# Up-projection in quads: the two B22 products of two pairs by seven sub-products of 256 columns

## The chip, the cores and the metric

The kernel runs on one core of a Trainium2 chip. Its engines are TensorE (PE in the profile; PEld are its weight loads), VectorE (DVE), ScalarE (ACT), GpSimd (Pool) and SyncE (SP), which issues most of the DMAs. Each engine works its own queue of instructions in order and waits on semaphores for the others. The metric is the device time of the core in microseconds: the median of the runs, lower is better.

## The reference

One layer of a hybrid encoder over 1024 tokens of 1024 channels. The change is in its last part, the gated feed-forward network:

```python
def conv_gated_ffn(x, w_up, conv_w, conv_b, w_down):
    hu = x @ w_up                                   # 1024x1024 @ 1024x5632
    hc = conv_b + conv_w[2] * hu                    # causal depthwise conv, width 3
    for i in range(2):
        hc = hc + conv_w[i] * shift(hu, 2 - i)
    val, gate = jnp.split(hc, 2, axis=-1)
    return (jax.nn.gelu(gate, approximate=True) * val) @ w_down
```

## The kernel before

All arithmetic is float32. A float32 product is made of three matmuls: each operand is split into a high part (an fp32r copy, made by ACT, `wh`) and the low remainder (a subtraction on VectorE, `wl`), both in `split` (L78), and `mm3` (L84) issues high x high, high x low and low x high for each tile of 128 channels (a "k tile"). The weights are the stationary operand, the tokens the moving one.

The up-projection is worked in 22 pairs. A pair g is 128 value columns and the 128 gate columns that belong to them. Its 1024 x 256 weights and the 1024 x 1024 activations are each taken as a 2 x 2 block matrix, and the product is made by seven products of blocks in place of eight (`Pair`, `p1` to `p7`, in Winograd's form). The blocks of activations are B11, B21 and B22, the sums of them are T1 to T4; the sums of weights are s1 to s4. Each product has four k tiles, so 12 matmuls of 128 x 128 weights over 512 tokens, into one PSUM bank. `p3` is the product of s4 with B22: it is added in bank Y, to what p5 left there, and evicted with u2.

The order of a pair is p1, p2, p6, p3, p7, then p5 of the next pair, then p4 (`run_pair`). The weights' sums are made by `first` (s1) and `sums` (s2, s4, s3), on VectorE for g below 7 and on GpSimd from there (`V if g < 7 else G`). The splits run on ACT and VectorE a product or more ahead. Evictions to `hu` (L1183) are additions on VectorE, u2 (L260) and the copies of p1 and p5 are ACT's. After a pair, `conv` takes `hu` through an ACT pass (L1234) and two conv steps on VectorE (L1239); `gate` takes the GELU on ACT (L1244) and the product on VectorE (L1245), and stores to `g_d` in DRAM (the last two by a GpSimd DMA, the others by SP).

The start is written out by hand: pairs 0 and 1, whose first products run ahead, and p1 and p2 of pairs 2, 3 and 4, made ahead with results parked in DRAM (`e_d`), while the normalised activations `q` are turned in place into T1 to T4. Then comes the sequence 5, 2, 6, 3, 7, 4, 8, ... 21. A scheduler of the framework decides, at build time, where each instruction stands in its engine's queue; `tc.high_priority` and `tc.issue_after` steer it.

The down-projection (`prod(X, a11, b11, "p1", ...)` and on) follows on the same banks of TensorE. Its first products, p1, begin while the last pair is still gated; its p2 needs the loads a12 and b21, which SP issues (L1155) behind the loads that wait for gate 21's store.

Of the kernel before, what the change touches and what calls it, by code (L numbers as in the profile page):

```python
# [45 lines left out]
def trunk(ctx, tc, xn, xt, w_first, w_in, cols, gain_pre, bias, w_ao, w_pg, w_po, w_o, gains, w_up, w_dn, out):  # L46
# [1116 lines left out]
    with ExitStack() as ph:  # L1163
# [78 lines left out]
        def gate(g):  # L1242
# [8 lines left out]
        for at, g in enumerate(seq):  # L1251
            for n in seq[at + 1:at + 3]:
                if n not in raws and at:
                    load_wup(n)
            if at == NG - 4:
                for c in range(3):
                    load_chunk("a11", c)
            elif at >= NG - 2:
                load_chunk("b11", at - NG + 2)
            if g == 0:  # L1260
                new_hu(0)
                new_hu(1)
# [297 lines left out]
```

## Time and profile before

| | before |
|---|---|
| median of 3 runs | 1236.88 us (1236.60 to 1236.89) |
| profiled execution, span from first to last instruction | 1234.9 us |
| runs above that span | 2.0 us by the median (1236.88 - 1234.9); no other time of that execution is recorded |
| TensorE clock granted, mean | 0.998 |
| TensorE matmuls | 5743 |
| up-projection on TensorE | about 595 to 1017 us of the span |
| down-projection | from 1017.41 us on |

How to read the rows that follow in the prediction: a page row of a group gives line, engine, operation, tiles out<-in (buffer numbers left out), shape and count, then the busy time in us, the mean of one in ns, and the idle time ahead of it with what ended it. A row of the timeline gives start and duration in us. A row of stretches gives from:to, length, and the busy time and count of PE, PEld, DVE, ACT and POOL, then the granted clock, the share of the DMA engines and GB/s. Matmuls are pipelined, so their pace is the distance of their starts, not their durations; the same holds for short operations on VectorE.

### The profile page before, as it was taken

The page shows a single profiled execution, that of the slowest core. Times are in us where ns is not written, and L with a number is a line of the kernel's source. Part 1 is how long each engine was busy: PE and PEld are TensorE (multiplying, and loading weights), DVE is VectorE, ACT ScalarE, POOL GpSimd, SP SyncE. Part 2 cuts the span into 40 slices and gives each one's busy share as a digit, 9 for nine tenths or more (in the row PEclk, how much of TensorE's full clock was granted, in tenths as well). Part 3 has the DMA queues.
Part 4 walks back from the last instruction along what each step waited for, and adds up shares of the span by engine and source line. Part 5 has one row for each costly group of instructions (what it writes and reads, how often), then busy time and mean ns, then how long its engine had stood idle before and what let it go on. Part 6 is the DMA issues. An engine that isn't in the chain of part 4 may idle for free.

```text
span 1234.9 us, 16242 instructions
## 1 busy us (share of the span) xinstructions
PE 1225.3 (99%) x5743; PEld 1020.9 (83%) x5743; DVE 949.6 (77%) x1551; ACT 667.2 (54%) x1171; POOL 211.0 (17%) x183
## 2 busy tenths in 40 slices
PE   9999999999999999999999999999999999999997
PEld 7888888888889987888888888888888888888886
DVE  5898677866788878756799887667666675999968
ACT  6764355555577773434546555554545455445553
POOL 0000000043254545000000112433333300000000
PEclk9999999999999999999999999999999999999999
DMA  9879245438886845322352232222132127902103
GB/s 329 333 256 350 85 147 207 154 124 264 291 276 214 264 178 207 137 86 76 113 196 111 111 145 103 71 84 102 52 102 85 61 68 255 350 18 103 34 1 137
DMA packets 63857, 193.84 MB, mean 157 GB/s; under 512 B 6048, under 2 KB 6688, under 8 KB 58656
## 3 DMA queue, kind: packets, MB, share of 16 engines
q1 hardware_dynamic: 55712, 176.55, 40.8%
q10 hardware_dynamic: 7056, 12.59, 2.7%
q0 software_dynamic: 1008, 3.67, 0.7%
q8 instruction: 45, 0.74, 0.2%
q14 instruction: 36, 0.29, 0.1%
HBM read 139.84 MB, written 52.95 MB: 156 GB/s over the span
## 4 chain that ended last, share of the span: by engine, by line
PE 92%; DVE 6%; issue 1%; DMA 0%; ACT 0%; POOL 0%; DVEq 0%; ACTq 0%
PE X_u L84 19%; PE X_i L84 12%; PE Y_u L84 10%; PE Y_i L84 9%; PE X L84 7%; PE wops L1115 7%; PE Z_u L84 4%; PE y L84 4%; PE ybp L84 4%; PE Y L84 4%; PE f L916 3%; PE tp L891 2%; PE Z_i L84 2%; PE first L466 2%; PE pst L848 1%; DVE a L1405 1%
## 5 line engine op out<-in xcount | busy, mean ns | idle before, releaser
L1239 DVE SCALAR_TENSOR_TENSOR hc<-hu,cv,hc 128x1022 f32<-128x1022 f32 (+1 forms) x88 | 115.6, 1315 | 27.7 <-ACT hc L1234 27.7
L78 ACT CAST wh_u<-s_u 128x512 fp32r<-128x512 f32 x88 | 54.4, 619 | 90.2 <-PE Y_u L84 47.7
L78 DVE TENSOR_TENSOR wl_u<-s_u,wh_u 128x512 fp32r<-128x512 f32 x88 | 62.4, 711 | 33.9 <-ACT wh_u L78 33.9
L78 ACT CAST wh_i<-s_i 128x512 fp32r<-128x512 f32 x64 | 39.8, 622 | 75.9 <-PE X_i L84 36.0
L78 ACT CAST wh_u<-wup 128x512 fp32r<-128x512 f32 x60 | 37.3, 621 | 52.0 <-PE X_u L84 27.5
L78 DVE TENSOR_TENSOR wl_i<-s_i,wh_i 128x512 fp32r<-128x512 f32 x64 | 46.2, 722 | 21.3 <-ACT wh_i L78 16.3
L1234 ACT ACTIVATE hc<-hu,cv 128x1024 f32<-128x1024 f32 x44 | 54.6, 1244 | 9.8 <-DVE hu L1183 8.9
L202 POOL TENSOR_TENSOR s_i<-win 128x512 f32<-128x512 f32 x4 | 5.9, 1481 | 257.0 <-DVE wl_i L78 246.6
L202 POOL TENSOR_TENSOR s_u<-wup 128x512 f32<-128x512 f32 x15 | 25.7, 1713 | 139.4 <-DVE wl_u L78 139.4
L78 DVE TENSOR_TENSOR ptl<-tp,pth 128x512 fp32r<-128x512 f32 (+3 forms) x80 | 42.8, 552 | 7.7 <-ACT pth L78 7.2
L866 ACT ACTIVATE pe<-sm,st 128x640 f32<-128x640 f32 (+2 forms) x64 | 44.3, 695 | 7.7 <-DVE st L864 7.5
L870 POOL TENSOR_SCALAR pe<-pe,st 128x640 f32<-128x640 f32 (+4 forms) x58 | 40.7, 705 | 44.2 <-DVE st L868 30.0
L78 ACT CAST pth<-tp 128x512 fp32r<-128x512 f32 (+3 forms) x80 | 36.3, 474 | 15.9 <-PE tp L891 11.0
L78 DVE TENSOR_TENSOR wl_u<-wup,wh_u 128x512 fp32r<-128x512 f32 x60 | 43.0, 719 | 1.2 <-ACT wh_u L78 0.5
L84 PE MATMUL ybp<-mx,wh_yb 128*128 128x512 f32 x128 | 43.3, 412 | 0.0
L1244 ACT ACTIVATE hc<-hc 128x1024 f32<-128x1024 f32 x22 | 23.4, 1062 | 36.9 <-DVE hc L1239 36.9
L864 DVE CUSTOM_DVE_ANT_0 sm<-pst,bt 128x640 f32<-128x640 f32 (+2 forms) x64 | 40.7, 651 | 3.0 <-issue 1.7
L206 POOL TENSOR_TENSOR s_u<-s_u,wup 128x512 f32<-128x512 f32 x15 | 19.4, 1291 | 102.3 <-DVE wl_u L78 99.6
L916 PE MATMUL f<-pth,vv 128*128 128x256 f32 x144 | 36.6, 286 | 0.0
L916 PE MATMUL f<-ptl,vv 128*128 128x256 f32 x144 | 36.5, 287 | 0.0
L208 POOL TENSOR_TENSOR s_u<-wup 128x512 f32<-128x512 f32 x15 | 32.2, 2144 | 23.5 <-DVE wl_u L78 23.5
L891 PE MATMUL tp<-ident,pe 128*128 128x128 f32 x240 | 35.3, 274 | 0.2
(523 smaller groups left out, 4135.7 us busy)
## 6 DMA issues: line engine op xcount, KB each, us to landing
wup<-in_w_up SPq DMA_DIRECT2D x22, 1024.0 KB, 5.0
win<-in_w_in SPq DMA_DIRECT2D x16, 1024.0 KB, 7.0
g_d<-hc SPq DMA_DIRECT2D x20, 512.0 KB, 2.6
sig_d<-d ACTq DMA_DIRECT2D x32, 256.0 KB, 2.0
a<-g_d SPq DMA_DIRECT2D x8, 1024.0 KB, 11.4
b<-in_w_dn SPq DMA_DIRECT2D x8, 1024.0 KB, 12.7
w<-in_w_in SPq DMA_DIRECT2D x12, 512.0 KB, 7.3
x<-in_xn SPq DMA_DIRECT2D x8, 512.0 KB, 8.5
```

What stands on the lines that cost most here:

```text
L78: return A.copy(hi, src), (eng or V).tensor_tensor(lo, src, hi.bitcast(F32), ALU.subtract)
L84: nc.tensor.matmul(ps, a[i], b[i], start=start and i == 0 and p == 0, stop=stop and i == n - 1 and p == 2, skip_group_check=True,)
L202: self.eng.tensor_tensor(self.s1, self.w21, self.w22, ALU.add)
L208: self.eng.tensor_tensor(self.s3, self.w11, self.w21, ALU.subtract)
L864: V.tensor_tensor_reduce(so, sv, bv, -1.0, 3e38, ALU.add, ALU.min, st[:, 0:1])
L866: A.activation(pe[:, :n], sm[:, :n], AF.Exp, scale=-1.0, bias=st[:, 0:1], accum_out=st[:, 1:2])
L870: (V if 4 * h + J in (0, 1, 31) else G).tensor_scalar(pe[:, :n], pe[:, :n], st[:, 2:3], 1.0, ALU.mult, ALU.mult)
L891: nc.tensor.transpose(tp[:, c * P:(c + 1) * P], pe[:, b * P:(b + 1) * P], ident)
L916: nc.tensor.matmul(fo, vv[:, kb, e].rearrange("p a d -> p (a d)"), t[:, s], start=s == slots[0] and x == 0, stop=s == slots[-1] and x == 1)
L1115: nc.tensor.matmul(ps[:, 512 * c:512 * c + 512], a[k // 4][:, k % 4, sl], wo[k][b][:, 512 * c:512 * c + 512], start=k == 0 and x == 0, sto ...
L1234: A.activation(c, hu, AF.Identity, scale=cv[:, C_CW + 88 + b:C_CW + 89 + b], bias=cv[:, C_CB + b:C_CB + b + 1])
L1239: V.scalar_tensor_tensor(c[:, n:], hu[:, :S - n], cv[:, w:w + 1], c[:, n:], ALU.mult, ALU.add)
```

## The change

Pairs are worked two at a time, in quads: (0,1), (5,2), (6,3), (7,4), (8,9) ... (20,21). The order in a quad of pairs a and b is p1 a, p2 a, p1 b, p2 b, p6 a, p6 b, then both p3, then p7 a, p7 b, p5 of the next quad's two pairs, p4 a, p4 b. Pairs 2, 3 and 4 have no p1 and p2 there.

The two products s4(a) B22 and s4(b) B22 together are a 2 x 2 block product of their own: two rows of weights (a, b), two halves of channels (two k tiles each), two halves of tokens (256 columns each). In quads 1 to 9 they are made by seven sub-products of two k tiles and 256 columns, six matmuls each (`third`), 42 matmuls where there were 24 of 512. The right operands are quarters of B22 and of a new operand E22, whose four quarters are differences of quarters of B22, made once on GpSimd (`quarters`) and split once on ACT and VectorE, in two `raw` buffers. The left operands are halves of s4 of a and b (splits q3a, and q3d for a half) and four sums of such halves (`third_weights`, `third_sums`, each of 256 columns on GpSimd), split again (q3e, q3b). Four sub-products go directly into the banks Y of a and b; three go into two further banks (r, q), are copied to `cc` by ACT, and added to both u2 by GpSimd (L1298, L1301) and VectorE (L1304, from the bank). The first and the last quad keep `p3`.

`sums` writes s3 over w21, and `fourth` s4 over w12, so a pair has tiles of its own for s1 and s2 only. `cc` shares the three buffers of `hc`. The weights of pairs 5 and 2 are loaded over q[0,0] and q[1,1] once these are free; afterwards both pairs of the next quad are loaded at the start of a quad. The conv and gate calls of both pairs of a quad stand in the next quad; those of pairs 20 and 21 stand at the end. The parked p1 of pairs 2, 3 and 4 is loaded one pair at a time.

```diff
+            def sums(self):
+                self.s2 = self.st("s2")
+                self.eng.tensor_tensor(self.s2, self.s1, self.w11, ALU.subtract)
+                self.s3 = self.w21
+                self.eng.tensor_tensor(self.s3, self.w11, self.w21, ALU.subtract)
+            def fourth(self):
+                self.s4 = self.w12
+                self.eng.tensor_tensor(self.s4, self.w12, self.s2, ALU.subtract)
...
+        def load_over(g, t):
+            raws[g] = t.rearrange("p k n -> p (k n)")
+            nc.sync.dma_start(raws[g], w_up[g])
...
+        def third_weights(a, b):
+            A4, B4 = a.s4, b.s4
+            wA = split_w(A4, f"q3a_{a.name}")
+            wt = [wsp.tile([P, 4, P], F32R, tag=x, name=f"{x}_q3d_{a.name}") for x in ("wh", "wl")]
+            w22 = [x[:, 0:2] for x in wt]
+            split(w22[0], w22[1], B4[:, 2:4])
+            G.tensor_tensor(B4[:, 2:4], B4[:, 0:2], B4[:, 2:4], ALU.add)
+            return wA, w22
+        def third_sums(a, b):
+            A4, B4 = a.s4, b.s4
+            G.tensor_tensor(B4[:, 0:2], A4[:, 0:2], B4[:, 0:2], ALU.subtract)
+            G.tensor_tensor(A4[:, 0:2], B4[:, 2:4], A4[:, 0:2], ALU.subtract)
+            G.tensor_tensor(A4[:, 2:4], A4[:, 2:4], A4[:, 0:2], ALU.subtract)
+        def third(a, b, wA, w22):
+            wA2 = split_w(a.s4, f"q3e_{a.name}")
+            wB2 = split_w(b.s4, f"q3b_{a.name}")
+            w11, w12 = [[x[:, i:i + 2] for x in wA] for i in (0, 2)]
+            s2, s4 = [[x[:, i:i + 2] for x in wA2] for i in (0, 2)]
+            s3, s1 = [[x[:, i:i + 2] for x in wB2] for i in (0, 2)]
+            B, E = Tu["B22"], Tu["E22"]
+            r, q7 = [psu.tile([P, 512], F32, tag="m", name=f"{n}_{a.name}")[:, :256] for n in ("r", "q")]
+            cc = tmp.tile([P, 4, 256], F32, tag="hc", name=f"cc_{a.name}", bufs=3)
+            u2 = a.quad["u2"]
+            two = u2.rearrange("p f (c n) -> p f c n", c=2)
+            lo, hi = slice(0, 256), slice(256, 512)
+            eighths(r, w11, quarter(B, "11"), True, True)
+            with tc.high_priority():
+                A.copy(cc[:, 0], r)
+            eighths(b.Y[:, lo], w22, quarter(E, "21"), False, True)
+            eighths(a.Y[:, lo], w12, quarter(B, "21"), False, True)
+            eighths(r, s2, quarter(E, "22"), False, True)
+            with tc.high_priority():
+                A.copy(cc[:, 1], r)
+            G.tensor_tensor(two[:, :, 0], two[:, :, 0], cc[:, 0:2], ALU.add)
+            eighths(q7, s3, quarter(E, "12"), True, True)
+            A.copy(cc[:, 2], q7)
+            G.tensor_tensor(two[:, 1], two[:, 1], cc[:, 2:3].to_broadcast([P, 2, 256]), ALU.add)
+            eighths(a.Y[:, hi], s4, quarter(B, "22"), False, True)
+            eighths(r, s1, quarter(E, "11"), False, True)
+            V.tensor_tensor(two[:, :, 1], two[:, :, 1], r.unsqueeze(1).to_broadcast([P, 2, 256]), ALU.add)
+            a.evict(0, 1, a.Y, a.u2)
+            b.evict(0, 1, b.Y, b.u2)
...
+        quarters = [q[1, 1][:, k:k + 2, c:c + 256] for k in (0, 2) for c in (0, 256)]
+        for o, x, y in ((0, 1, 0), (1, 3, 1), (3, 3, 0), (2, 2, 3)):
+            G.tensor_tensor(quarters[o], quarters[x], quarters[y], ALU.subtract)
...
+        e22 = [rawp.tile([P, 4, 512], F32R, tag="raw", name=f"E22{x}") for x in "hl"]
+        for c in range(4):
+            split(e22[0][:, c], e22[1][:, c], q[1, 1][:, c])
+        Tu["E22"] = e22
+        load_over(2, q[1, 1])
+        p0.p7(False)
+        pair = pair_up(5), es[2]
+        pair[0].first()
...
+            a.p1()
+            if n == 1:
+                with tc.issue_after(gate(0).ins):
+                    for g in nxt:
+                        load_wup(g)
+                conv(1, 0)
+            else:
+                conv(u, 1)
+            a.p2()
+            a.fourth()
+            if n == 1:
+                conv(1, 1)
+            else:
+                gate(u)
+                conv(v, 1)
+            if not begun:
+                b.p1()
+                b.p2()
+            if n == 1:
+                b.first()
+                b.sums()
+                b.p5()
+            b.fourth()
+            a.p6()
+            gate(v)
+            if not final:
+                wts = third_weights(a, b)
+                third_sums(a, b)
+            b.p6()
+            if final:
+                a.p3()
+                b.p3()
+            else:
+                third(a, b, *wts)
+                after = []
+                for g in nxt:
+                    if g in es:
+                        es[g].weights(raws[g])
+                    after.append(es[g] if g in es else pair_up(g))
+                after[0].first()
+            a.p7(False)
+            conv(gs[0], 0)
+            if not final:
+                after[0].sums()
+                after[1].first()
+            b.p7(False)
+            if not final:
+                after[0].p5()
+                after[1].sums()
+                conv(gs[1], 0)
+                after[1].p5()
+            else:
+                conv(gs[1], 0)
+            a.p4(False)
+            if final:
+                conv(gs[0], 1)
+                gate(gs[0])
+            b.p4(False)
```

The first place is VectorE at the entry of quad 1. The names: u5 and u2 are the pairs, `wup2` or `h2_11` hold pair 2's weights, `h2_00` pair 5's; a name ends in a buffer's number. Before, from the low half of s2 of pair 5 (wl_6_u5, for its p6) to that of s1 of pair 2 (wl_5_u2, for its p5):

```order
L78 TENSOR_TENSOR wl_6_u5_6620<-s2_u5_6495,wh_6_u5_6619 128x512
L78 TENSOR_TENSOR wl_3_u5_6640<-s4_u5_6496,wh_3_u5_6639 128x512
L1245 TENSOR_TENSOR hc0_0_6554<-hc0_0_6554,hc0_1_6558 128x1024
L78 TENSOR_TENSOR wl_7_u5_6657<-s3_u5_6497,wh_7_u5_6656 128x512
L1183 TENSOR_TENSOR hu5_0_6613<-Z_u5_6596,p1_u5_6567 128x512
L206 TENSOR_TENSOR s2_u2_6677<-s1_u2_6616,wup2_6562 128x512
L1239 SCALAR_TENSOR_TENSOR hc1_1_6592<-hu1_1_6129,cv_76,hc1_1_6592 128x1022
L207 TENSOR_TENSOR s4_u2_6678<-wup2_6562,s2_u2_6677 128x512
L1239 SCALAR_TENSOR_TENSOR hc1_1_6592<-hu1_1_6129,cv_76,hc1_1_6592 128x1023
L208 TENSOR_TENSOR s3_u2_6679<-wup2_6562 128x512
L78 TENSOR_TENSOR wl_5_u2_6686<-s1_u2_6616,wh_5_u2_6685 128x512
```

And now the rows from pair 5's s4 to gate 1's product:

```order
L1215 TENSOR_TENSOR h2_00_5305<-h2_00_5305,s2_u5_6502 128x512
L202 TENSOR_TENSOR s1_u2_6624<-h2_11_5308 128x512
L1364 TENSOR_TENSOR hc0_0_6558<-hc0_0_6558,hc0_1_6562 128x1024
L1209 TENSOR_TENSOR s2_u2_6626<-s1_u2_6624,h2_11_5308 128x512
L1183 TENSOR_TENSOR hu5_0_6617<-X_u5_6600,p1_u5_6571 128x512
L1211 TENSOR_TENSOR h2_11_5308<-h2_11_5308 128x512
L1358 SCALAR_TENSOR_TENSOR hc1_1_6620<-hu1_1_6129,cv_76,hc1_1_6620 128x1022
L78 TENSOR_TENSOR wl_5_u2_6632<-s1_u2_6624,wh_5_u2_6631 128x512
L1358 SCALAR_TENSOR_TENSOR hc1_1_6620<-hu1_1_6129,cv_76,hc1_1_6620 128x1023
L1215 TENSOR_TENSOR h2_11_5308<-h2_11_5308,s2_u2_6626 128x512
L78 TENSOR_TENSOR wl_6_u5_6651<-s2_u5_6502,wh_6_u5_6650 128x512
L1364 TENSOR_TENSOR hc1_0_6596<-hc1_0_6596,hc1_1_6620 128x1024
```

wl_5_u2 stood ten rows behind wl_6_u5 and stands three ahead of it; s1, s2 and s3 of pair 2 moved ahead of it with it.

The second place is GpSimd in the steady part, one quad. Before, the s1, s2, s4 and s3 of pair 9 (L202, L206, L207, L208), and on with pair 10 in the same pattern:

```order
L202 TENSOR_TENSOR s1_u9_7402<-wup9_7243 128x512
L206 TENSOR_TENSOR s2_u9_7463<-s1_u9_7402,wup9_7243 128x512
L207 TENSOR_TENSOR s4_u9_7464<-wup9_7243,s2_u9_7463 128x512
L208 TENSOR_TENSOR s3_u9_7465<-wup9_7243 128x512
L202 TENSOR_TENSOR s1_u10_7550<-wup10_7357 128x512
```

And now, in quad (10, 11), up to its last two operations (L1209 is s2, L1215 s4, L1211 s3, L1267 to L1275 the sums of the halves of s4; u12 and u13 are the next quad's pairs):

```order
L202 TENSOR_TENSOR s1_u12_8018<-wup12_7814 128x512
L1211 TENSOR_TENSOR wup12_7814<-wup12_7814 128x512
L1215 TENSOR_TENSOR wup11_7486<-wup11_7486,s2_u11_7754 128x512
L1209 TENSOR_TENSOR s2_u12_8042<-s1_u12_8018,wup12_7814 128x512
L1267 TENSOR_TENSOR wup11_7486<-wup11_7486 128x256
L1273 TENSOR_TENSOR wup11_7486<-wup10_7484,wup11_7486 128x256
L1274 TENSOR_TENSOR wup10_7484<-wup11_7486,wup10_7484 128x256
L1275 TENSOR_TENSOR wup10_7484<-wup10_7484 128x256
L202 TENSOR_TENSOR s1_u13_8045<-wup13_7816 128x512
L1211 TENSOR_TENSOR wup13_7816<-wup13_7816 128x512
L1298 TENSOR_TENSOR u2_u10_7907<-u2_u10_7907,cc_u10_7967 128x2x256
L1301 TENSOR_TENSOR u2_u10_7907<-u2_u10_7907,cc_u10_7967 128x512
```

The sums of halves and the two additions to u2 (L1298, L1301) came in between, the latter behind s1 and s3 of the next quad's second pair.

The third place is VectorE at the end of the up-projection, from the last conv step of the last gate's half to that gate's product; p1a and p1b are operands of the down-projection's p1. Before, of pair 21:

```order
L1239 SCALAR_TENSOR_TENSOR hc21_1_9427<-hu21_1_9330,cv_76,hc21_1_9427 128x1022
L1239 SCALAR_TENSOR_TENSOR hc21_1_9427<-hu21_1_9330,cv_76,hc21_1_9427 128x1023
L78 TENSOR_TENSOR wl_p1a2_9521<-a11_0_8839,wh_p1a2_9520 128x512
L78 TENSOR_TENSOR wl_p1a3_9541<-a11_0_8839,wh_p1a3_9540 128x512
L1245 TENSOR_TENSOR hc21_0_9389<-hc21_0_9389,hc21_1_9427 128x1024
```

And now, beginning with the last conv step and the product of gate 20:

```order
L1358 SCALAR_TENSOR_TENSOR hc20_1_9696<-hu20_1_9651,cv_76,hc20_1_9696 128x1023
L1364 TENSOR_TENSOR hc20_0_9653<-hc20_0_9653,hc20_1_9696 128x1024
L78 TENSOR_TENSOR wl_p1a2_9830<-a11_0_9138,wh_p1a2_9829 128x512
L78 TENSOR_TENSOR wl_p1a3_9850<-a11_0_9138,wh_p1a3_9849 128x512
L1358 SCALAR_TENSOR_TENSOR hc21_1_9736<-hu21_1_9673,cv_76,hc21_1_9736 128x1022
L78 TENSOR_TENSOR wl_p1a4_9870<-a11_1_9140,wh_p1a4_9869 128x512
L1358 SCALAR_TENSOR_TENSOR hc21_1_9736<-hu21_1_9673,cv_76,hc21_1_9736 128x1023
L78 TENSOR_TENSOR wl_p1a5_9890<-a11_1_9140,wh_p1a5_9889 128x512
L78 TENSOR_TENSOR wl_p1a6_9910<-a11_1_9140,wh_p1a6_9909 128x512
L78 TENSOR_TENSOR bl_p1b4_9874<-b11_1_9472,bh_p1b4_9873 128x512
L1364 TENSOR_TENSOR hc21_0_9675<-hc21_0_9675,hc21_1_9736 128x1024
```

Gate 20's product and five more splits of the down-projection stand ahead of gate 21's product now, one of them, bl_p1b4, for that p1's fifth k tile.

More of the change, by code (lines that the diff above doesn't have):

```diff
@@ L1231, in conv @@
             b = g + NG * f
-            hu = hus[g][f]
+            hu = hus[g, f]
             c = hcs[g, f] = tmp.tile([P, S], F32, tag="hc", name=f"hc{g}_{f}", bufs=3)
@@ L1367, in trunk @@
+            if not final:
+                pair = after
+        with tc.high_priority():
+            pre = [(split_a(blk["a11"][k], f"p1a{k}"), split_a(blk["b11"][k], f"p1b{k}")) for k in range(2)]
+        conv(gs[1], 1)
+        gate(gs[1])
     upp.close()
```

265 lines of the change are left out of this document (147 added, 118 removed).

## Prediction

> **What bounds the kernel now.** I read the page's busy times first, then the chain that ended last, then busy times by stretch.
>
> ```profile
> span 1234.9 us, 16242 instructions
> PE 1225.3 (99%) x5743; PEld 1020.9 (83%) x5743; DVE 949.6 (77%) x1551; ACT 667.2 (54%) x1171; POOL 211.0 (17%) x183
> ...
> PE 92%; DVE 6%; issue 1%; DMA 0%; ACT 0%; POOL 0%; DVEq 0%; ACTq 0%
> ...
> 595.00:1017.00 422.00, 421.97 (x1873) 348.93 (x1872) 323.40 (x391) 227.42 (x330) 98.99 (x62) 1.00 0.28 97
> 640.00:660.00 20.00, 20.00 (x90) 16.57 (x89) 19.73 (x27) 10.14 (x14) 0.00 (x0) 1.00 0.49 177
> 660.00:680.00 20.00, 20.00 (x90) 16.57 (x89) 19.89 (x27) 11.05 (x17) 0.00 (x0) 1.00 0.35 122
> 680.00:700.00 20.00, 20.00 (x90) 16.58 (x89) 17.73 (x22) 11.55 (x18) 1.28 (x1) 1.00 0.28 106
> 760.00:798.00 38.00, 38.00 (x169) 31.46 (x168) 25.55 (x30) 19.45 (x29) 13.29 (x9) 1.00 0.24 83
> ```
>
> The columns of a stretch are its length, then the busy time of PE, PEld, DVE, ACT and POOL. TensorE makes 99% of the span, and in the up-projection (595 to 1017 us) it idles 0.03 us in 422, at full clock (1.00). So a matmul that goes is time that goes, as long as nothing starts to be late. How much the others have left differs by stretch: from 760 on, two pairs take 38 us and VectorE has 12.5 us free; between 640 and 680, where pairs 0 and 1 run out and pair 5 begins, VectorE has 0.38 us free in 40. The two stretches are judged apart.
>
> **The matmuls: removed 24, added 42, per quad.** The start times of a 12-matmul product (its first matmul, and that of the next product), then two rows each of two runs of 256-column matmuls in the attention, which load new weights for each matmul as the new ones do (PEld has as many instructions as PE):
>
> ```profile
> 837.89 0.39 PE L84 MATMUL Y_u<-B22h,wh_u 128*128 128x512 f32 x1
> ...
> 840.61 0.39 PE L84 MATMUL X_u<-T3h,wh_u 128*128 128x512 f32 x1
> 439.64 0.28 PE L916 MATMUL f<-ptl,vv 128*128 128x256 f32 x1
> ...
> 440.78 0.28 PE L916 MATMUL f<-ptl,vv 128*128 128x256 f32 x1
> 376.19 0.28 PE L916 MATMUL f<-pth,vv 128*128 128x256 f32 x1
> ...
> 377.49 0.28 PE L916 MATMUL f<-ptl,vv 128*128 128x256 f32 x1
> ```
>
> A product takes 2.72 us, 0.227 a matmul. The first run has ten distances in 1.14 us (0.114), the second eleven in 1.30 (0.118); I take 0.116. Two products were 5.44 us; 42 matmuls are 42 x 0.116 = 4.87 us: 0.57 us less. Quads 1 to 9 are worked so (the first and the last keep p3): 9 x 0.57 = **5.2 us gained**; by 0.118 it is 4.4, by 0.114 5.9. From 0.130 on nothing is gained.
>
> **The start, quad 1 (pairs 5 and 2).** Pair 2's s1, s2, s3 and product p5 now stand ahead of pair 5's p6; before, p5 came three products (8 us) later, behind pair 5's p6, p3 and p7. Four splits of E22 (four 512-column subtractions on VectorE) come before them, and the load of pair 2's weights, on SP, waits for these. VectorE's durations:
>
> ```profile
> 640.20 0.68 DVE L258 TENSOR_TENSOR u_u<-X_u,hu 128x512 f32<-128x512 f32 x1
> 640.80 0.68 DVE L202 TENSOR_TENSOR s_u<-wup 128x512 f32<-128x512 f32 x1
> ...
> 652.58 3.67 DVE L1239 SCALAR_TENSOR_TENSOR hc<-hu,cv,hc 128x1022 f32<-128x1022 f32 x3
> 656.16 0.69 DVE L1183 TENSOR_TENSOR hu<-X_u,hu 128x512 f32<-128x512 f32 x1
> ...
> 659.16 1.22 DVE L1245 TENSOR_TENSOR hc<-hc,hc 128x1024 f32<-128x1024 f32 x1
> 660.29 0.68 DVE L78 TENSOR_TENSOR wl_u<-s_u,wh_u 128x512 fp32r<-128x512 f32 x1
> 661.05 0.69 DVE L1183 TENSOR_TENSOR hu<-Z_u,p_u 128x512 f32<-128x512 f32 x1
> ...
> 665.85 0.68 DVE L78 TENSOR_TENSOR wl_u<-s_u,wh_u 128x512 fp32r<-128x512 f32 x1
> ```
>
> From start to start a 512-column operation takes 0.60, a conv step 1.19 (3.58 / 3), a gate product 1.13. After the operation of 640.20 the new queue holds, up to and with wl_5 of pair 2, 23 operations of 512 (four of them E22), seven conv steps and one gate product: 23 x 0.60 + 7 x 1.19 + 1.13 = 23.3 us from 640.8, so wl_5 is there at 664.1 (before: 666.5, the row of 665.85). TensorE ends pair 5's p2 at about 660.9 (the eviction of 661.05 waited for it). Its new order fills in with two matmuls of each of four products whose high half is there (2 x 0.227 + 2 x 0.227 + 4 x 0.116 = 1.4), until 662.3, and then waits for wl_5: **1.8 us**. Next, ten matmuls later (666.4), it needs wl_6 of pair 5, which stands behind a conv step and two more operations: 664.1 + 1.19 + 3 x 0.60 = 667.1 at most; I take 0.2 for it, as each operation's result counts from its own end. Sum **2.0 us lost, once**. Nothing gives it back: TensorE has no later idle time. Ends: 0 (if VectorE runs these in another rhythm), 5.5 (the new Pool sums at their slowest, 4 x 0.98 us later than I count, below, which would make wl_q3e late). I stay at the queue's sum. The third's splits come in time by this count: wl_q3d ends at 668.8, Pool's four sums of 256 columns take half of L206's 1.29 each (671.4), ACT and VectorE some 0.6 each with a start between (672.8); wl_q3e is wanted at 673.2, after pair 2's p6 (671.6) and the sub-products ahead. The c1 halves are now loaded one by one (three of 256 KB); the DMA queues were busy 0.35 to 0.49 there, so I cost that at nothing.
>
> **The steady quads.** Per quad come 1.5 splits, three copies of 256 columns on ACT, one addition with PSUM on VectorE (L1304), and on Pool four operations of 256 and two of 512 columns (L1298, L1301). VectorE's 1.5 x 0.60 + 0.60 = 1.5 us go into 12.5 us of free time; ACT's into 18. Pool's are the question, since L1298 and L1301 stand in a chain: copy of r, L1298, L1301, L1304, and behind L1304 on VectorE everything that leads to wl_4.
>
> ```profile
> L206 POOL TENSOR_TENSOR s_u<-s_u,wup 128x512 f32<-128x512 f32 x15 | 19.4, 1291 | 102.3 <-DVE wl_u L78 99.6
> L202 POOL TENSOR_TENSOR s_u<-wup 128x512 f32<-128x512 f32 x15 | 25.7, 1713 | 139.4 <-DVE wl_u L78 139.4
> L208 POOL TENSOR_TENSOR s_u<-wup 128x512 f32<-128x512 f32 x15 | 32.2, 2144 | 23.5 <-DVE wl_u L78 23.5
> 664.07 0.58 ACT L260 COPY u_u<-X_u 128x512 f32<-128x512 f32 x1
> ```
>
> Count from a.p1 (T = 0), with products of 2.72: six products and the third's first four sub-products (24 x 0.116) end at 19.1, the copy of r at most 0.58 later, 19.7. L1298 and L1301 at 1.29 each: 22.3. L1304 22.9; wl_5 of the next pair, two evictions and that of a.p7, 4 x 0.60: 25.3; ACT's conv of a began after the first of these evictions (24.1) and takes 1.25 (the page's L1234 group has a mean of 1244 ns, quoted below), so conv step a 25.4 to 26.6; conv step b, an eviction, two conv steps and wl_4: 26.6 + 1.19 + 0.60 + 2.38 + 0.60 = 31.4; with hand-overs of some 0.05 us I take 31.7. TensorE wants wl_4 at 21.2 + 4 x 2.72 + 2 x 0.227 = 32.5. **Margin 0.8 us, cost 0.** Of the Pool rows I take L206's, since L1298 too waits for another engine and is then free to start; behind it in Pool's queue stand L1301 and the next pair's s2 and s4, wanted many us later. Ends: no loss, or both operations as long as L208's (2.14, at single rows 2.27): 2 x 0.98 - 0.8 = 1.2 us a quad, 10.4 in all. Why L208 is slow:
>
> ```profile
> L1234 ACT ACTIVATE hc<-hu,cv 128x1024 f32<-128x1024 f32 x44 | 54.6, 1244 | 9.8 <-DVE hu L1183 8.9
> 796.25 2.27 POOL L208 TENSOR_TENSOR s_u<-wup 128x512 f32<-128x512 f32 x1 [1.76 <-DVE wl_u L78]
> ...
> 796.09 1.27 DVE L1239 SCALAR_TENSOR_TENSOR hc<-hu,cv,hc 128x1023 f32<-128x1023 f32 x1
> ```
>
> It starts 0.16 us into a conv step on VectorE, which ends at 797.36, and takes 1.16 us from there: as if it had waited for that end. In the new order wl_7 and wl_5 splits stand on VectorE at T = 19 to 22, not conv steps, and they wait for TensorE; so a Pool operation can meet one of 0.6 us. [...]
>
> **The tail.** Gates 20 and 21 both come at the end, and SP's loads of the down-projection stand behind them.
>
> ```profile
> 1017.41 0.39 PE L84 MATMUL X<-wh_p1b,wh_p1a 128*128 128x512 f32 x1
> ...
> 1023.63 1.22 DVE L1245 TENSOR_TENSOR hc<-hc,hc 128x1024 f32<-128x1024 f32 x1
> ...
> 1032.32 0.92 SPq L1155 DMA_DIRECT2D a<-g_d  x2
> ...
> 1039.75 0.62 ACT L78 CAST wh_p2a<-a 128x512 fp32r<-128x512 f32 x1 [2.15 <-DMA a<-g_d]
> ...
> 1047.37 0.39 PE L84 MATMUL Y<-bh_p2b,wh_p2a 128*128 128x512 f32 x1
> ```
>
> Gate 21's product came 6.2 us after the down-projection's start; by the new queue (gate 20, two splits, a conv step, a split, a conv step, three splits ahead of it) it comes at about 11. The store and the loads behind it, b21 and a12, move 4.9 us with it: a12 is there at 1044.6, split by 1046.0, wanted at 1047.4. Cost **0**, margin 1.4; the other end is 2.
>
> **Sum**, against the profiled execution: span 1234.9 - 5.2 + 2.0 = 1231.7 us. The runs' median, 1236.88, lies 2.0 above that span; the same lies around the new one: **1233.7 us**.
>
> **Rivals.** *Pool in the chain (slower).* Decides from a loss of 3.2 / 9 = 0.36 us a quad, i.e. when L1298 and L1301 take over 1.29 + (0.8 + 0.36) / 2 = 1.87 us each. At L208's 2.27 the time is 1233.7 + 10.4 = 1244.1. For it: two of the three Pool rows are above 1.7. Against: what stands beside them on VectorE. *Half of it (no change).* At 1.8 us each: 2 x 0.51 - 0.8 = 0.2 a quad, 2 us; with a further 1 us at quad 1 or in the tail, 1236.7. For it: three places with margins of 0.4 to 1.4 us. *The narrow matmuls do not do what they say.* If 42 loads of weights, each before only 256 columns, do not hide, the distance is above 0.130 and nothing is gained: 1236.9 + 2.0 = 1238.9. At PEld's mean of 178 ns (1020.9 / 5743) it would be 42 x 0.178 - 5.44 = 2.0 us more a quad, 1257. Against: both quoted runs. [...]
>
> **Chances.** Forecast 0.5, Pool 0.18, half of it 0.22, narrow matmuls 0.1. What differs by under 0.2% (2.5 us) cannot be told from no change here. The forecast's gain is 3.2, so a fifth of its cases count as no change, and of the half case and of the narrow matmuls a fourth as slower: faster 0.40, same 0.35 (0.1 + 0.17 + 0.08), slower 0.25. The range goes from 1231 (0.114, and nothing lost at the start) to 1241 (two thirds of the Pool case).
>
> **What would show it.** Right: 256-column matmuls at L84 0.114 to 0.118 apart; one idle time of about 2 us of TensorE near 662, waiting for wl_u of VectorE; none in the later quads; Pool's L1298 and L1301 at 1.3. Wrong: idle time of TensorE before p4 in each quad (Pool case), before p2 of the down-projection (tail), or distances above 0.12.

## The result and the profile after

| | before | after |
|---|---|---|
| median | 1236.60 us (1236.35 to 1236.89, 5 runs) | 1266.23 us (1264.24 to 1268.86, 5 runs) |
| ratio | | 1.0238, 95% interval 1.0225 to 1.0250 |
| profiled execution, span | 1234.9 us | 1267.1 us |
| mean granted clock | 0.998 | 0.993 |

The kernel became 29.6 us slower, on the side that the forecast gave 0.25, and outside its range. The profiled execution is the slowest of the five after (1268.86), so its span is 32.2 us longer than before. The page of the kernel after (busy times, the chain's shares by engine):

```profile
PE 1235.6 (98%) x5905; PEld 1027.7 (81%) x5905; DVE 1008.4 (80%) x1581; ACT 683.9 (54%) x1220; POOL 281.6 (22%) x241
...
PE 76%; DVE 12%; issue 5%; ACT 5%; DMA 1%; POOL 1%; DVEq 0%; SPq 0%; ACTq 0%; POOLq 0%
```

The same stretches as before:

```profile
595.00:1017.00 422.00, 400.32 (x1894) 330.09 (x1893) 355.59 (x389) 224.33 (x352) 166.27 (x118) 0.98 0.24 90
660.00:680.00 20.00, 16.06 (x81) 13.18 (x81) 18.68 (x25) 11.62 (x18) 4.33 (x4) 1.00 0.43 159
680.00:700.00 20.00, 20.00 (x91) 17.09 (x90) 17.81 (x23) 10.25 (x16) 4.29 (x3) 0.91 0.31 109
760.00:798.00 38.00, 36.23 (x177) 29.93 (x176) 29.84 (x32) 20.55 (x33) 18.30 (x14) 1.00 0.22 83
```

TensorE, which idled 0.03 us of 422 before, now idles 21.7. From 680 to 700 it is busy throughout, but its granted clock is 0.91. VectorE was not full: from 760 to 798 it has 8 us free. The waits of TensorE from 595 to 1060 us (what it waited for, sum, times, longest):

```profile
PE Z_u L84 <- DVE wl_u L78: 4.7, 5, 1.6
PE X_u L84 <- DVE wl_u L78: 4.1, 6, 1.2
PE Z_u L84 <- ACT p_u L1223: 3.0, 1, 3.0
PE X_u L84 <- ACT p_u L1223: 2.3, 1, 2.3
PE Y_u L84 <- DVE wl_u L78: 2.2, 1, 2.2
PE Y_u L84 <- DVE p_u L215: 2.0, 2, 1.2
PE r_u L84 <- ACT cc_u L1292: 1.7, 1, 1.7
```

No single wait carries the loss: there are low halves (`wl_u`), two copies of p1 (L1223), evictions and the copy of r (L1292). A steady quad, from one p4 to that of the next quad (the timeline's starts of two matmuls), before:

```profile
884.13 0.39 PE L84 MATMUL X_u<-T4h,wh_u 128*128 128x512 f32 x1
...
922.21 0.39 PE L84 MATMUL X_u<-T4h,wh_u 128*128 128x512 f32 x1
```

and after:

```profile
890.72 0.39 PE L84 MATMUL X_u<-T4h,wh_u 128*128 128x512 f32 x1
...
930.81 0.39 PE L84 MATMUL Z_u<-T4h,wh_u 128*128 128x512 f32 x1
```

38.08 us became 40.09: 2.0 us more, where 0.57 less was forecast.

To compare kernels I sum, for each quad, how far the starts of its matmuls lie apart beyond 0.2267 us (512 columns: a product of before, 2.72 us, by 12) or half of it, 0.1134 (256): its **loss**. It holds waits, a lower clock and wider spacing alike. With it, a third that loses nothing saves 24 x 0.2267 - 42 x 0.1134 = 0.68 us. Quad 0 is pairs 0 and 1; quads 1 to 3 are pairs 5, 2, 6, 3, 7, 4; 4 to 9 are the steady ones. The rows below `after` are the experiments that follow.

| kernel | median us | quad 0 | 1 | 2 | 3 | each of 4 to 9 (mean) |
|---|---|---|---|---|---|---|
| before | 1236.6 | 0.7 | 0 | 0 | 0 | 0 |
| after | 1266.2 | 3.8 | 6.5 | 4.5 | 6.0 | 3.0 |
| e1_p3all | 1237.5 | 1.3 | 0 | 0 | 0 | 0 |
| e4_p3pool | 1241.8 | 3.9 | 0.6 | 1.2 | 0.6 | 0 |
| e3_nopool | 1252.7 | 1.3 | 2.6 | 4.4 | 3.0 | 1.9 |
| e2_vec | 1260.8 | 3.1 | 5.6 | 2.8 | 3.9 | 2.6 |
| e5_prep6 | 1285.2 | 3.9 | 5.8 | 7.4 | 6.4 | 5.4 |
| e10_gate | 1262.8 | 3.8 | 6.0 | 4.3 | 4.9 | 2.5 |
| e12_behind | 1257.7 | 3.9 | 4.8 | 6.2 | 6.5 | 1.5 |
| e13_q4 | 1249.0 | 3.9 | 2.1 | 0 | 0 | 1.8 |
| e14_q4_p4off | 1247.4 | 3.9 | 2.2 | 0 | 0 | 1.4 |
| e15_q4_p54 | 1239.9 | 3.9 | 2.1 | 0 | 0 | 0.4 |

For the kernel after, 3.8 + 6.5 + 4.5 + 6.0 + 6 x 3.0 = 39 us lost, less 9 x 0.68 = 6.1 saved and 0.7 that before lost too, is 32: the difference of the spans.

Five of the six steady quads lose 2.7 us, one (from 808 us on) 4.7. In the five, 1.95 us of the loss stand in the second p6 (T2), 0.45 at p4 (T4), 0.27 in the third. The timeline there, ACT first, then VectorE, then TensorE (start, duration, idle time ahead and its releaser):

```profile
945.23 0.60 ACT L78 CAST wh_q3a_u<-wup 128x512 fp32r<-128x512 f32 x1
945.74 0.40 ACT L78 CAST wh_q3d_u<-wup 128x256 fp32r<-128x256 f32 x1
...
948.99 1.06 ACT L1363 ACTIVATE hc<-hc 128x1024 f32<-128x1024 f32 x1 [2.37 <-DVE hc L1358]
949.96 0.60 ACT L78 CAST wh_u<-s_u 128x512 fp32r<-128x512 f32 x1
...
950.09 1.23 DVE L1364 TENSOR_TENSOR hc<-hc,hc 128x1024 f32<-128x1024 f32 x1 [0.85 <-ACT hc L1363]
951.23 0.68 DVE L1183 TENSOR_TENSOR hu<-Z_u,p_u 128x512 f32<-128x512 f32 x1
951.83 0.68 DVE L78 TENSOR_TENSOR wl_u<-s_u,wh_u 128x512 fp32r<-128x512 f32 x1
...
950.61 0.50 PE L84 MATMUL X_u<-T2h,wh_u 128*128 128x512 f32 x1 [0.16 <-ACT wh_u L78]
...
952.56 0.50 PE L84 MATMUL X_u<-T2h,wl_u 128*128 128x512 f32 x1 [1.22 <-DVE wl_u L78]
```

The splits q3a and q3d of the third went ahead, and the split of b's s2 (949.96, 951.83) came to stand behind gate(v): its GELU (948.99), which itself waited for a conv step, and its product (950.09). ACT sat idle 2.37 us ahead of that GELU while TensorE was about to run out of weights.

### The profile page after: what moved, and what is told of

The parts are those of the page before. It is cut to its first block, busy times and chain, and to the rows that moved or that the text cites. A ratio compares the mean times of both kernels' runs of the same rounds, so it can differ in the third digit from the quotient of the medians.

```text
span 1267.1 us, 16734 instructions
## 1 busy us (share of the span) xinstructions
PE 1235.6 (98%) x5905; PEld 1027.7 (81%) x5905; DVE 1008.4 (80%) x1581; ACT 683.9 (54%) x1220; POOL 281.6 (22%) x241
## 4 chain that ended last, share of the span: by engine, by line
PE 76%; DVE 12%; issue 5%; ACT 5%; DMA 1%; POOL 1%; DVEq 0%; SPq 0%; ACTq 0%; POOLq 0%
PE X_i L84 12%; PE X L84 9%; PE Y_i L84 9%; PE Y L84 7%; PE wops L1115 7%; DVE hc L1358 5%; PE X_u L84 4%; PE Z_u L84 4%; PE y L84 4%; PE ybp L84 3%; PE f L916 3%; DVE wl_u L78 3%; PE Y_u L84 2%; PE tp L891 2%; ACT hc L1353 2%
## 5 line engine op out<-in xcount | busy, mean ns | idle before, releaser
L1358 DVE SCALAR_TENSOR_TENSOR hc<-hu,cv,hc 128x1022 f32<-128x1022 f32 (+1 forms) x88 | 125.0, 1439 | 14.1 <-ACT hc L1353 12.4
L78 ACT CAST wh_u<-wup 128x512 fp32r<-128x512 f32 x80 | 48.7, 619 | 49.9 <-PE Y_u L84 19.6
L1353 ACT ACTIVATE hc<-hu,cv 128x1024 f32<-128x1024 f32 x44 | 53.7, 1242 | 36.2 <-DVE hu L1183 31.9
L78 DVE TENSOR_TENSOR wl_u<-wup,wh_u 128x512 fp32r<-128x512 f32 x80 | 59.3, 771 | 12.0 <-ACT wh_u L78 11.8
L202 POOL TENSOR_TENSOR s_i<-win 128x512 f32<-128x512 f32 x4 | 6.3, 1584 | 257.8 <-DVE wl_i L78 246.8
L78 DVE TENSOR_TENSOR wl_u<-s_u,wh_u 128x512 fp32r<-128x512 f32 x44 | 46.4, 1054 | 11.6 <-ACT wh_u L78 11.5
L1363 ACT ACTIVATE hc<-hc 128x1024 f32<-128x1024 f32 x22 | 23.3, 1061 | 53.7 <-DVE hc L1358 50.9
L1215 POOL TENSOR_TENSOR wup<-wup,s_u 128x512 f32<-128x512 f32 x15 | 25.6, 1709 | 88.7 <-DVE wl_u L78 88.7
L1364 DVE TENSOR_TENSOR hc<-hc,hc 128x1024 f32<-128x1024 f32 x22 | 29.4, 1338 | 17.9 <-ACT hc L1363 17.9
L84 PE MATMUL Y_u<-T1h,wl_u 128*128 128x512 f32 x88 | 34.3, 390 | 2.2 <-DVE wl_u L78 2.2
L78 ACT CAST wh_u<-s_u 128x512 fp32r<-128x512 f32 x44 | 27.1, 617 | 16.9 <-DVE s_u L202 5.6
```

Of the source, the lines that this page charges most:

```text
L78: return A.copy(hi, src), (eng or V).tensor_tensor(lo, src, hi.bitcast(F32), ALU.subtract)
L84: nc.tensor.matmul(ps, a[i], b[i], start=start and i == 0 and p == 0, stop=stop and i == n - 1 and p == 2, skip_group_check=True,)
L1215: self.eng.tensor_tensor(self.s4, self.w12, self.s2, ALU.subtract)
L1353: A.activation(c, hu, AF.Identity, scale=cv[:, C_CW + 88 + b:C_CW + 89 + b], bias=cv[:, C_CB + b:C_CB + b + 1])
L1358: V.scalar_tensor_tensor(c[:, n:], hu[:, :S - n], cv[:, w:w + 1], c[:, n:], ALU.mult, ALU.add)
L1364: V.tensor_tensor(val, val, gt, ALU.mult)
```

## The experiments

Four theories. **A**: Pool's new operations and VectorE hold each other up. **B**: the new order of calls for two pairs at once, with the gates in other places, without the third. **C**: the added splits and sums fill ACT and VectorE. **D**, formed after the first four runs: not the amount, but what stands ahead of a split in ACT's and VectorE's queues.

**The order of quads without the third.** Every quad computes its B22 products by p3, and E22 and all new Pool operations go:

```diff
-            if not final:
-                wts = third_weights(a, b)
-                third_sums(a, b)
...
-            if final:
-                a.p3()
-                b.p3()
-            else:
-                third(a, b, *wts)
+            a.p3()
+            b.p3()
+            if not final:
```

> The quad order with p3 kept in every quad: no sub-products, no E22, none of the new GpSimd operations; all the rest as changed. Theory A (GpSimd's and VectorE's operations on two SBUF inputs hold each other up, and the new GpSimd operations so make VectorE's queue late): 1234 to 1242 us. Theory B (the order: two convs and gates in a row ahead of the split for the second p6, whatever GpSimd does): over 1255. Theory C (the added splits and additions fill VectorE and ACT): as A, 1234 to 1242.

1237.52 us, ratio 1.0007 (0.9998 to 1.0017). No loss from quad 1 on. The order of quads costs nothing that can be told from no change; B falls. In this kernel the split of b's s2 stands ahead of gate(v): on ACT (below) ahead of the GELU, on VectorE at 916.99, ahead of the gate's product (920.50). TensorE wants it at about 922.4.

```profile
915.13 0.60 ACT L78 CAST wh_u<-s_u 128x512 fp32r<-128x512 f32 x1
...
918.96 1.06 ACT L1363 ACTIVATE hc<-hc 128x1024 f32<-128x1024 f32 x1 [0.88 <-DVE hc L1358]
```

**Pool's operations alone.** p3 everywhere as above, but Pool does `quarters` and as many operations of the same size in each quad, into a scratch tile that nobody reads:

```diff
+                for c in range(4):
+                    G.tensor_tensor(scr[:, 0], a.s4[:, 0:2], b.s4[:, 2:4], ALU.add)
...
+                for c in range(2):
+                    G.tensor_tensor(scr.rearrange("p a k n -> p (a k n)"), u2s[:, 0], u2s[:, 1], ALU.add)
```

> As e1 (p3 in every quad), with as many GpSimd operations of the same sizes as the change adds, at the same places, into a scratch tile that nobody reads (and the quarters made, but not split). A: they alone bring 10 us or more over e1: 1248 to 1262. B and C: the time of e1 within 2 us.

1241.82 us, 1.0043 (1.0028 to 1.0058): 4.3 us above the run without them (A expected 10 or more, B and C at most 2), 2.6 of it in quad 0, none in the steady quads. Quad 0, in the kernel after (Pool, VectorE, TensorE):

```profile
625.08 8.36 POOL L1431 TENSOR_TENSOR h<-h 128x512 f32<-128x512 f32 x4 [22.14 <-ACT p_u L1328]
...
626.85 1.52 DVE L78 TENSOR_TENSOR wl_u<-s_u,wh_u 128x512 fp32r<-128x512 f32 x1 [0.17 <-ACT wh_u L78]
628.30 1.78 DVE L1209 TENSOR_TENSOR s_u<-s_u,wup 128x512 f32<-128x512 f32 x1
630.00 2.31 DVE L78 TENSOR_TENSOR T3l<-h,T3h 128x1024 fp32r<-128x1024 f32 x1
632.23 0.68 DVE L215 TENSOR_TENSOR p_u<-Y_u,hu 128x512 f32<-128x512 f32 x1
...
634.51 1.21 DVE L78 TENSOR_TENSOR T3l<-h,T3h 128x1024 fp32r<-128x1024 f32 x1
...
633.05 0.47 PE L84 MATMUL Y_u<-B22h,wh_u 128*128 128x512 f32 x1 [1.23 <-DVE p_u L215]
```

While Pool works on `quarters`, three operations of VectorE take 0.84, 1.10 and 1.10 us longer than their like outside (0.68, 0.68, 1.21), and the eviction L215 that TensorE waits for comes late. A holds here, and for 4 us.

**Pool's operations left out, and moved to VectorE.** The first takes all six from each quad and `quarters`; the second makes each `G.tensor_tensor` of them a `V.tensor_tensor` (one of them shown):

```diff
-        G.tensor_tensor(B4[:, 0:2], A4[:, 0:2], B4[:, 0:2], ALU.subtract)
+        V.tensor_tensor(B4[:, 0:2], A4[:, 0:2], B4[:, 0:2], ALU.subtract)
```

> The changed kernel without the new GpSimd operations at all (the quarters, the sums of the halves of s4 and the additions to u2 are left out; all matmuls, splits and copies stay). A: 1232 to 1242. B and C: over 1255, since order, splits and copies are all there.

> The changed kernel with the new GpSimd operations (the four quarters of E22, the four sums per quad, L1298 and L1301) on VectorE. A: the mutual holding goes, VectorE has 2.6 us more a quad: 1240 to 1250. B: as changed, 1263 to 1269. C: slower than changed, over 1269.

Without them 1252.68 (1.0132, 1.0117 to 1.0147), on VectorE 1260.75 (1.0187, 1.0170 to 1.0204); neither lies in a range that a theory gave. So 13.6 of the 29.6 us need Pool's operations or what waits for them; but 16 us stay without any, and the T2 loss of a steady quad is still 1.6 us. A explains a part; C and D remain.

**b's split ahead of the gate.** D as first stated:

```diff
             a.p6()
+            b.prep("6", b.s2)
             gate(v)
```

> The changed kernel with one line more: the split of b's s2 (for b.p6) is called ahead of gate(v) and third_weights, so that it does not stand behind the splits q3a and q3d and gate v's product. Theory D (the calls' order: the third's splits took the places of that split, which so fell behind the gate): the stall of 1.95 us in p6 of quads 4 to 9 goes to 0.3 or less, 10 to 13 us in all with quads 2, 3 and 5: 1252 to 1257. Theory C (VectorE and ACT are too full): it reappears at the next split, 1262 or more. Theory A (GpSimd): the same as changed, 1263 to 1269.

1285.19 us, 1.0387 (1.0372 to 1.0403). The T2 loss of the steady quads went to 0 as expected, but the third now lost 3.8 to 6.5 us a quad, as C had it: the loss came up again at the next split. VectorE, Pool, ACT and TensorE of that kernel:

```profile
962.48 2.31 DVE L1364 TENSOR_TENSOR hc<-hc,hc 128x1024 f32<-128x1024 f32 x1
964.71 0.68 DVE L1183 TENSOR_TENSOR hu<-Z_u,p_u 128x512 f32<-128x512 f32 x1
965.31 0.41 DVE L78 TENSOR_TENSOR wl_q3d_u<-wup,wh_q3d_u 128x256 fp32r<-128x256 f32 x1
...
965.80 0.73 POOL L1267 TENSOR_TENSOR wup<-wup 128x256 f32<-128x256 f32 x1 [2.10 <-DVE wl_q3d_u L78]
...
969.00 0.62 ACT L78 CAST wh_q3e_u<-wup 128x512 fp32r<-128x512 f32 x1 [4.93 <-POOL wup L1275]
...
970.94 0.39 PE L84 MATMUL r_u<-E22h,wh_q3e_u 128*128 128x256 f32 x1 [2.64 <-ACT cc_u L1292]
```

Now q3d stood behind the gate's product (962.48, 2.31 us where a gate's product took 1.23 in the kernel after, 950.09), Pool's four sums behind q3d, wh_q3e behind these, and ACT's copy of r (L1292) behind wh_q3e in ACT's queue. The gate delays whichever split comes after it.

Three variants on top of this one left the loss of the steady quads (5.4, here 5.1 to 5.4 a quad): quad 1 by p3, e6_prep6_q1, 1278.95 (1.0337, 1.0321 to 1.0352); with the copy of p1 at high priority, e7_prep6_q1_c1, 1278.59 (1.0333, 1.0318 to 1.0349); with `quarters` on VectorE too, e9_e7_qv, 1280.28 (1.0346, 1.0328 to 1.0363).

> As e5_prep6, and quad 1 keeps p3 (the sub-products start with quad 2). By the idle time of quad 1 in the changed kernel (6.5 us, 5.9 of it in the third) it should be 5 to 6 us under e5_prep6 if the stall was the third's own inputs there; if it was VectorE being late from the start on, it moves on into quad 2 and 0 to 2 us are gained.

> As e6_prep6_q1, and the ACT copy of p1 at high priority. The changed kernel loses 2.4 and 3.2 us in quads 2 and 3 to this copy, which stands behind a gate's GELU on ACT. If its place in the queue is the cause: 4 to 5 us under e6. If the GELU is late because VectorE is late, and the copy only the next in line: 0 to 2.

> As e7, with the four quarters of E22 made on VectorE in place of GpSimd (8.4 us there, 2.1 each). Theory A for the start: the stall of 2.35 us in p6 of pairs 0 and 1 goes, VectorE has 2.4 us more: 0 to 2 us under e7. Theory C: slower than e7 by 1 to 3.

Quad 1 by p3 lost 2.1 us in place of 5.8. That also ended quad 2's loss at p2 (2.3); with the copy of p1 ahead of the GELU, quad 3's fell only from 3.4 to 2.9. `quarters` on VectorE lost 1.7 us at quad 1's p5 and 1.8 in quad 0's p7 and p4, in place of the 2.4 at its p6: no way round.

**All splits ahead of the gate.** gate(v) is issued behind ACT's copy of a's p6:

```diff
             a.p6()
-            gate(v)
             if not final:
                 wts = third_weights(a, b)
                 third_sums(a, b)
+            b.prep("6", b.s2)
+            with tc.issue_after(a.copied.ins):
+                gate(v)
             b.p6()
```

> The kernel after, with the call order changed at one place of the loop: third_weights, third_sums and b.prep("6") come before gate(v), and gate(v) is issued only behind ACT's copy of a's p6 to u2. So wl_q3a, wl_q3d and wl_6_b all stand ahead of gate(v)'s product on VectorE. Theory D (what costs the steady quads some 2.7 us each is that whichever of these splits goes last stands behind gate(v)'s GELU and product): the loss at T2 and at the third product of quads 4 and 6 to 9 goes below 1 us per quad, in all 10 to 16 us less than the kernel after: 1250 to 1256. Theory C (the added splits fill VectorE and ACT, so that something is late in any order) and theory A (the POOL sums stretch VectorE): the loss moves to another product but stays, 1260 to 1270.

1262.83 us, 1.0210 (1.0193 to 1.0227): 3.4 us less than after, not 10 to 16. T2 lost 0 to 0.1 in the later quads; the third lost 1.7, p4 0.7. The same GELU stood ahead of ACT's copy of r, for which TensorE waited 0.88 us (until 951.31):

```profile
948.93 1.06 ACT L1363 ACTIVATE hc<-hc 128x1024 f32<-128x1024 f32 x1
949.89 0.61 ACT L78 CAST wh_q3b_u<-wup 128x512 fp32r<-128x512 f32 x1
...
950.87 0.39 ACT L1292 COPY cc_u<-r_u 128x256 f32<-128x256 f32 x1
```

The same with quad 1 by p3 and the copy of p1 at high priority:

> The former run with two more edits: quad 1 computes its B22 products by p3 for each pair, without the third, and ACT's copy of p1 into c1 is issued at high priority, ahead of the GELU. Theory D with the local losses of quads 1 to 3 on top: 6.5 us of quad 1 less, since its third waits for wl_5_u2 and cc_u, and 2 us each of quads 2 and 3, so 8 to 10 us below the former run: 1240 to 1247, still not below the kernel before, since the quads that remain gain 0.4 us each (8 of them, 3.2 us) and quad 0 loses 3. Theory C: no more than 3 us below the former run.

1258.53 us, 1.0173 (1.0158 to 1.0189): 4.3 us below, where 8 to 10 were expected. Quad 1's loss fell from 6.0 to 2.2 and quad 2's from 4.3 to 1.7, but quad 3 took 1.1 more.

**The gate behind the third's copies.** In the last four kernels `a.copied` is the second copy of r where a quad has the third, and gate(v) is issued behind it (elsewhere behind the copy of a's p6):

```diff
-            if final:
+            if not final:
+                third(a, b, *wts)
+                with tc.issue_after(a.copied.ins):
+                    gate(v)
+            else:
                 a.p3()
                 b.p3()
-            else:
-                third(a, b, *wts)
...
```

> e10_gate with gate(v) issued still later: behind ACT's second copy of r into cc_u (L1297), so that wh_q3e, wh_q3b and both copies of r on ACT, and all six splits on VectorE, stand ahead of the GELU and its product. In e10_gate T2's loss of 1.95 us per quad was gone, and the third lost 1.7 instead: its first copy of r stood behind that GELU on ACT (948.93, 1.06 us), then wl_q3b behind the product. Theory D (one GELU and one product of 128x1024, wherever they stand ahead of what the quad's second p6 or its third need): the third's loss in quads 4 to 9 goes to 0.3 or less, T4's may grow from 0.7 to 1.5; 1262.8 less 6 x 1.4 = 8 us, 1253 to 1257. Theory C (too much work on ACT and VectorE in that stretch in any order): the loss moves to T3 or T4 in full, 1261 to 1265.

> e12_behind with the B22 products of quads 1 to 3 by p3 (the third from quad 4 on, in 6 quads), the copy of p1 ahead of the GELU, and a's split for p4 called ahead of conv(gs[1], 0). Theory D: no loss is left in quads 1 to 3 and 0.3 us in each of quads 4 to 9, which just spends the 0.4 us that a third saves; quad 0 keeps the 2.6 us that POOL's quarters cost it: 1237 to 1241, level with the kernel before or a little slower. If T4's loss moves with the split, down to 1236.5. Theory C: a loss of 1.5 us or more in each of the six quads, 1246 or more.

1257.74 (1.0172, 1.0157 to 1.0187) and 1248.95 (1.0099, 1.0082 to 1.0116). In the first, the third's loss went to 0.57 and p4's rose to 0.9 (0.45 in the kernel after): wl_4 waits behind the four conv steps of a and b, which now start late. VectorE of e12_behind:

```profile
957.72 2.46 DVE L1358 SCALAR_TENSOR_TENSOR hc<-hu,cv,hc 128x1022 f32<-128x1022 f32 x2
960.11 0.68 DVE L1183 TENSOR_TENSOR hu<-X_u,p_u 128x512 f32<-128x512 f32 x1
960.71 2.46 DVE L1358 SCALAR_TENSOR_TENSOR hc<-hu,cv,hc 128x1023 f32<-128x1023 f32 x2
963.10 2.48 DVE L78 TENSOR_TENSOR wl_u<-wup,wh_u 128x512 fp32r<-128x512 f32 x4
```

In the second, with the condition `not final and n > 3` on the third and the copy of p1 at high priority, quads 2 and 3 lose nothing, and my own last edit, p4's split ahead of the conv, put b's wl_5 behind the same conv steps: 1.3 us a quad at p5. The two runs that follow take that edit back, and put both splits ahead:

```diff
                 after[1].sums()
+                after[1].prep("5", after[1].s1)
+                a.prep("4", a.w22)
                 conv(gs[1], 0)
                 after[1].p5()
```

> e13_q4 without its last edit: a's split for p4 is called where it was, behind conv(gs[1], 0). In e13_q4 T2 lost nothing in any later quad and the third 0.27 us (its matmuls' distance), but 1.3 us a quad had come up at the next pair's p5: wl_5 of b stood behind wl_4 and four conv steps. If that is the edit's doing alone: quads 4 to 9 lose 0.3 us each, 1248.95 - 6 x 1.4 = 1240.5. If the third itself makes the conv steps late (both pairs' Y come at its end, where p3 gave a's one product earlier), wl_4 is late in its place: 0.9 us a quad as in e12_behind, 1246 to 1247.

> e14_q4_p4off with the splits of the next pair's p5 and of a's p4 both called ahead of conv(gs[1], 0), in the order in which TensorE wants them. Theory D (order alone): nothing late at p5 or p4, 0.3 us a quad left, of which 0.4 is the third's own saving: 1239 to 1242. Theory C (VectorE has too much to do in any order): 0.8 us or more a quad at p4 or at p1 of the next pair, 1245 or more.

1247.35 (1.0085, 1.0071 to 1.0099), near the second of its two cases (1246 to 1247): p4 loses 0.9 again. And 1239.91 (1.0028, 1.0018 to 1.0038), within theory D's 1239 to 1242: in the steady quads only the third's 0.27 is left (0.7 in one of the six). From p4 to p4 in this kernel:

```profile
868.72 0.39 PE L84 MATMUL X_u<-T4h,wh_u 128*128 128x512 f32 x1
...
906.42 0.39 PE L84 MATMUL Z_u<-T4h,wh_u 128*128 128x512 f32 x1
```

and busy times in that stretch:

```profile
868.72:906.42 37.70, 37.70 (x188) 32.07 (x186) 29.99 (x34) 20.71 (x34) 20.43 (x14) 1.00 0.23 82
```

A quad takes 37.70 us, 0.38 less than before, with all the third's splits and Pool sums in it, and TensorE never idles. VectorE is busy 29.99 of these 37.70 us; in the kernel after it was 31.93 of 40.09 (from 890.72), the same share with as many operations. So its average load does not tell the two kernels apart, and the steady loss came with the order: C falls there. Until this run the totals had spoken for C as much as for D: e5_prep6, e10_gate and e13_q4 lie where C had them, and e11_gate_q1_c1 and e12_behind in neither range. The order also decides which operations of VectorE run beside Pool's, and the same operations are busy 1.9 us less here; how much of the steady loss was the place in the queue and how much such meetings is not separated.

Quads 2 and 3 lose nothing by p3, quad 1 2.1 us; no run has the third in quads 1 to 3 without a loss, so it is not shown that an order can take their loss away too.

No version beats the kernel before. This one keeps 3.2 us of quad 0 and 2.1 of quad 1; six thirds give 1.9. Whether E22 can be made elsewhere than in the start was not tried.

## Why the prediction was wrong

**The matmuls** were mis-sized. Start of the third's first matmul and of the product behind it, after:

```profile
954.96 0.28 PE L84 MATMUL r_u<-B22h,wh_q3a_u 128*128 128x256 f32 x1
...
959.99 0.40 PE L84 MATMUL X_u<-T3h,wh_u 128*128 128x512 f32 x1
```

Busy time and count of the weight loads (PEld) in that stretch:

```profile
954.96:959.99 5.03, 5.03 (x42) 1.00 0.00 0
```

5.03 / 42 = 0.120 each, not 0.116; 5.44 - 5.03 = 0.41 a quad and 3.7 in nine, not 5.2. The third rival had the direction, not the size. Its mechanism, loads that do not hide, stays open: the loads fill this stretch, but their records overlap (0.19 us each, 0.120 apart), and in the attention runs of the prediction loads of 0.19 us go 0.114 to 0.118 apart.

**The start.** The 1.8 us wait for wl_5 of pair 2 came at its place, as 2.20, and the queue's sum of 23.3 us held (from 644.39 to 667.72); TensorE and wl_5 both came some 3.5 us later than counted, as quad 0 lost 3.8 us, before 0.7:

```profile
667.86 0.50 PE L84 MATMUL Y_u<-T1h,wl_u 128*128 128x512 f32 x1 [2.20 <-DVE wl_u L78]
...
678.98 0.39 PE L84 MATMUL r_u<-E22h,wh_q3e_u 128*128 128x256 f32 x1 [1.74 <-ACT cc_u L1292]
```

The step that failed is "The third's splits come in time by this count". Pool's four sums took 1.06 to 1.13 us each, not the 0.65 that I made of half of L206, and ACT's queue was worked in order: the copy of r, whose matmuls had ended at about 676.2, began at 678.55, behind wh_q3e, which waited for them.

```profile
672.43 1.13 POOL L1267 TENSOR_TENSOR h<-h 128x256 f32<-128x256 f32 x1 [38.99 <-DVE wl_q3d_u L78]
...
677.03 0.62 ACT L78 CAST wh_q3e_u<-h 128x512 fp32r<-128x512 f32 x1 [3.58 <-POOL h L1275]
```

With the lower clock that followed (0.91 from 680 to 700 us), quad 1 lost 6.5 us, not 2.0; the end of 5.5 that I named for late Pool sums was nearer. Quads 2 and 3, where ACT's copy of p1 (L1223) stood behind a GELU for 2.3 and 3.0 us, I counted among the steady ones at nothing: 10.5 us. Quad 0, where `quarters` cost 2.6 (e4_p3pool against e1_p3all), had no term at all.

**The steady quads** are where the sign was lost. The chain that I worked out held nearly: L1298 and L1301 took 1.32 and 1.37 us in the mean (1.29 forecast), and p4 came 0.45 late in place of 0.8 early. What failed is "VectorE's 1.5 x 0.60 + 0.60 = 1.5 us go into 12.5 us of free time; ACT's into 18": I followed one chain, from r to wl_4, and put every other new instruction into an average. The free time of a queue that is worked in order is of no use to an operation that stands behind one that waits. With the third, b's s2 split came to stand behind gate(v), for whose GELU ACT sat idle 2.37 us, where e1_p3all has it ahead; e15_q4_p54, with the same work in another order, loses 0.4 a quad, of which 0.27 is the spacing of the third's matmuls. 18 us were lost here in all, forecast 0.

**The tail** held: from the first matmul of p1 of the down-projection to that of p2 it took 0.5 us more (30.44, before 29.96), and from that first matmul to the end of the span 217.5 us in both. Gate 21's product came 11.3 us after it (about 11 forecast); six splits stand ahead of that product now, two before, so four more, not the five named in "The change".

**The rivals.** "Pool in the chain" had the sign, by luck, and a time 22 us short; its place (L1298 and L1301 ahead of p4) was wrong, its durations too. That VectorE's operations can be held up while Pool works is shown by the rows of `quarters` (0.84 to 1.10 us on three of them); Pool's operations weigh 4.3 us by themselves (e4_p3pool against e1_p3all).

## What to carry to other kernels

Where the engine that bounds the kernel has no idle time, check every weight split that the change adds or moves, not one chain: for each, list what now stands ahead of it in its engine's queue and what that waits for. A long operation that waits for another engine (a GELU and its product) belongs behind all splits and copies that the bound engine needs next; here moving one split at a time only handed the wait on. And set a change's gain (0.4 us a quad) against the cost of one such wait (1.2 us) before judging it by sums of busy time.

## What was not expected of the hardware

A longer wait of TensorE can be paid twice. After the waits of quad 1 the granted clock was 0.91 in 680 to 700 us, and 256-column matmuls stood 0.213 us apart instead of 0.120 from 680.6 to 683.2, 1.5 us more with the start of the next product. The same distance followed the 2.64 us wait of e5_prep6, and a clock of 0.83 (830 to 840 us) a wait of 1.58 us in one steady quad of the kernel after (830.89), which makes that quad's 4.7; the 1.22 us waits of the other steady quads were followed by none. It does not follow every long wait: the one of 2.20 in quad 1 was followed by none before the next wait. By the starts of the up-projection's matmuls in all sixteen traces, a stretch of some 3 us at about half the pace (in the kernel after 0.213 us a matmul of 256 columns, 0.42 to 0.43 of 512) came within 1.7 us of 2 of 8 waits of 1.4 to 1.7 us, 8 of 20 of 1.7 to 2.3 us and 28 of 33 longer ones, and of none of 71 waits of 0.6 to 1.4 us. What sets such a stretch off is not shown.
